# Neighbourhood attention on half key blocks, with the query blocks in the order 1, 2, 0, 3

## The chip, the core and the metric

The kernel runs on one core of a Trainium2 chip. The metric is the device time of one execution in microseconds; the kernel before takes 1600.47 us (median of three runs, 1600.18 to 1600.92).

## What is computed

The reference is an encoder of two layers on 512 tokens of width 1024. In each layer a normed input goes through one combined projection and from there into four branches: a convolution branch, neighbourhood attention (NA), dilated attention and windowed attention; the branches are gated, summed, projected and added back, and a feed-forward part with a small convolution follows. The change touches the second branch. Cut to what matters of it:

```python
def _neighbourhood_attn(q, k, v, rpb):      # grid of 8 rows x 64 columns, 4 heads of 64
    ...
    col_start = np.clip(col - kc // 2, 0, GRID_W - kc)      # kc = 16
    col_idx = col_start[:, None] + np.arange(kc)[None, :]
    ...
        s = jnp.einsum('bwhd,brwkhd->bhwrk', q_r, k_r).astype(jnp.float32) * scale
        s = s + bias[None]
        p = jax.nn.softmax(s.reshape(bsz, heads, GRID_W, kr * kc), axis=-1)
        ...
        return jnp.einsum('bhwrk,brwkhd->bwhd', p, v_r)
```

A query sees the 16 nearest grid columns (clamped at the edges) with all 8 rows of each. The bias depends on the difference of rows and columns and on the head.

## The kernel before

The weights are streamed from memory once, in units of 128 x 1024. Each unit is loaded on the SP queue (`w_raw`, L201), split by ScalarE into a high part (`w_hi`, L204) and by VectorE into a low part (`w_lo`, L206), and multiplied in three products (L225 to L227, or L407 to L409 for projections with tokens on the partitions). There are two buffers for the raw unit and three for each part.

All attention work is put into this stream. The method `tick` is called at fixed places between products, and each call takes one step of the generators that wait in `side`. So TensorE's order is written out by the program: a stretch of weight products, one attention step, the next stretch.

For NA the tokens are kept column by column of the grid, 8 tokens to a column, so a block of 128 queries covers 16 grid columns and its keys lie in the neighbouring columns. `qk_norm` (L460) transposes Q and K and splits K into `KH` and `KL`. `project_v` (L543) evaluates V for two branches; NA's V is written to the DRAM buffer `turn` row by row (L552) and read back in grid order as one tile `Vn` of 1024 KB (L556), called V in the rows.

`attention` (L570) serves three branches. It has 16 items, one for each of 4 heads and 4 query blocks. At step t it does three things:

- `values` (L637), in every second step: for a pair of blocks (`hf`, blocks 0 and 1 or 2 and 3) it multiplies V with the transposed probabilities, a high product (L651) and a low one (L652) for each key block, into one PSUM tile; ScalarE copies the lower half out (L657) and VectorE adds the halves (L658, tile `yf`).
- `transposes` (L619) of item t-3: a transpose for each key block (L628), a copy into `pth` by ScalarE (L634) and the low part `ptl` by VectorE (L635).
- `scores` of item t (L581): two products, Q with `KH` (L591) and with `KL` (L592); VectorE adds the bias and takes the maximum (L605), ScalarE makes the exponential (L609) and the scaled copy (L616).

Score, transpose and value results share four PSUM buffers (`aux`, L219), which are taken in turn. So a score product may have to wait for the reader of a result that was made four buffers earlier.

Key ranges are whole blocks of 128: block i sees the blocks i-1 to i+1, so the inner blocks 1 and 2 have 384 keys and the outer ones 256. In `values` a pair reads three key blocks, the first two by 256 query columns or, for the third, the one block of 128 that sees it. The bias table of a head has 896 columns (L152): 384 that both inner blocks use, and 256 for each outer block. It is loaded into a single buffer `tab` of 448 KB at the head's first score step (L583 to L586):

```python
            if kind == 'na' and i == 0:
                tab = self.ap.tile([P, 896], F32, name="tab", tag="tab", bufs=1)
                nc.sync.dma_start(tab, self.TB[l, h])
                tabs[h] = tab
```

The order of instructions on each engine and queue is fixed when the program is built, and instructions of one engine run in that order.

Of the kernel before, what the change touches and what calls it, by code (L numbers as in the profile page):

```python
# [22 lines left out]
P = 128  # L23
L = 2
D = 1024
S = 512
KT = D // P
NB = S // P
# [117 lines left out]
def na_tables(rpb):  # L146

    c_of = np.arange(S) // 8
    r_of = np.arange(S) % 8
    parts = []  # L150
    pad = np.concatenate([rpb.reshape(L, 4, -1), np.full((L, 4, 1), -BIG, np.float32)], -1)
    for blk, k0, k1 in ((1, 0, 384), (0, 0, 256), (3, 256, 512)):  # L152
        q = blk * P + np.arange(P)
        k = np.arange(k0, k1)
        cq, rq, ck, rk = c_of[q][:, None], r_of[q][:, None], c_of[k][None], r_of[k][None]
        cs = np.clip(cq - 8, 0, 48)
        ok = (ck >= cs) & (ck < cs + 16)
# [23 lines left out]
class Trunk:  # L181
# [361 lines left out]
    def project_v(self, Vn, Vd):  # L543

        vn = [self.ap.tile([P, 2, 4, P], F32R, name=n, tag=n, bufs=2) for n in ("pth", "ptl")]
        turn = self.dram.tile([S // 8, 8, 4 * P], F32, name="turn", tag="turn", bufs=1)

        def evac(b, ps):
            t = vn[b // 2][:, b % 2]
            self.evac_v(t, b, ps[:, :256], 4)  # L550
            for e in range(2):
                self.nc.sync.dma_start(turn[:, 2 * b + e],  # L552
                                       t[64 * e:64 * e + 64].bitcast(F32).rearrange("p h x -> p (h x)"))
            self.evac_v(Vd[:, b], b, ps[:, 256:], 4)
        self.token_major(evac)
        self.nc.sync.dma_start(Vn.bitcast(F32).rearrange("p b h x -> p b (h x)"),  # L556
                               turn.rearrange("(b c) r x -> (c r) b x", b=NB))

    def project_swa(self, V):
        Q = self.new_Q()  # L560
# [9 lines left out]
    def attention(self, l, kind, V, yi):  # L570


        nc = self.nc
        v = nc.vector
        QS, KH, KL = self.qk
        yh, yl = self.y_tiles()
        half = lambda e: slice(64 * e, 64 * e + 64)
        blocks = lambda i: (0, 4) if kind == 'dil' else (max(0, i - 1), min(4, i + 2))
        tabs, yfs, pts = {}, {}, {}

        def scores(h, i):  # L581
            hk = h // 2 if kind == 'swa' else h
            if kind == 'na' and i == 0:  # L583
                tab = self.ap.tile([P, 896], F32, name="tab", tag="tab", bufs=1)
                nc.sync.dma_start(tab, self.TB[l, h])
                tabs[h] = tab  # L586
            k0, k1 = blocks(i)
            n = (k1 - k0) * P
            ps = self.aux()
            q = QS[:, h, i * P:(i + 1) * P]  # L590
            nc.tensor.matmul(ps[:, :n], lhsT=q, rhs=KH[:, hk, k0 * P:k1 * P], start=True, stop=False)  # L591
            nc.tensor.matmul(ps[:, :n], lhsT=q, rhs=KL[:, hk, k0 * P:k1 * P], start=False, stop=True)  # L592
            if kind == 'na':
                o = {0: 384, 3: 640}.get(i, 0)
                bias = tabs[h][:, o:o + n]
# [21 lines left out]
            return e  # L617

        def transposes(h, i, e):  # L619
            hf, u = i // 2, i % 2  # L620
# [3 lines left out]
            k0, k1 = blocks(i)  # L624
            n = (k1 - k0) * P
            ps = self.aux()
            for kb in range(k1 - k0):
# [3 lines left out]
            K0 = 0 if kind == 'dil' else hf  # L631
            ks = slice(k0 - K0, k1 - K0)
            qs = slice(u * P, (u + 1) * P)
            nc.scalar.activation(pth[:, ks, qs], src, AF.Copy)  # L634
            v.tensor_tensor(ptl[:, ks, qs], src, pth[:, ks, qs].bitcast(F32), ALU.subtract)  # L635

        def values(h, hf):  # L637
            hk = h // 2 if kind == 'swa' else h
            pth, ptl = pts.pop((h, hf))
            full = slice(0, 256)  # L640
            if kind == 'dil':
                K0, kbs = 0, [(kb, full) for kb in range(4)]
            else:

                K0, kbs = hf, [(0, full), (1, full), (2, slice(P, 256))]
                if hf == 1:
                    kbs = [(1, full), (2, full), (0, slice(0, P))]
            po = self.aux()
            for n, (kb, qs) in enumerate(kbs):
                vs = V[:, K0 + kb, hk, :]  # L650
                nc.tensor.matmul(po[:, qs], lhsT=vs, rhs=pth[:, kb, qs], start=n == 0, stop=False)  # L651
                nc.tensor.matmul(po[:, qs], lhsT=vs, rhs=ptl[:, kb, qs], start=False, stop=n == len(kbs) - 1)  # L652
            if h % 2 == 0 and hf == 0:
# [4 lines left out]
            v.tensor_tensor(yf[half(h % 2), hf * 256:(hf + 1) * 256], po[0:64, :256], tmp, ALU.add)  # L658
            if h % 2 == 1 and hf == 1:
                j = h // 2  # L660
                s_, oh, ol = yf, yh[:, j, :], yl[:, j, :]
# [3 lines left out]
                nc.scalar.activation(oh, s_, AF.Copy)  # L665
                v.tensor_tensor(ol, s_, oh.bitcast(F32), ALU.subtract)

        items = [(h, i) for h in range(4) for i in range(NB)]
        es, n = {}, len(items)
        for t in range(n + LAG + 2):  # L670
            if t >= LAG + 3 and (t - LAG) % 2 == 1:
                h, i = items[t - LAG - 3]
                values(h, i // 2)
# [198 lines left out]
    def layer(self, l):  # L872
# [3 lines left out]
        with tc.tile_pool(name="gate", bufs=1, reuse_waits="tile") as self.gp:  # L876
            with tc.tile_pool(name="attn", bufs=1, reuse_waits="tile") as self.ap:
                self.scratch = lambda: self.gp.tile([P, S], F32, name="raw", tag="t1", bufs=2)
                late = lambda n: iter([None] * n)
# [100 lines left out]
```

## Time and profile before

| What | Value |
|---|---|
| median of three runs | 1600.47 us (1600.18 to 1600.92) |
| profiled execution, its own time | 1601.61 us |
| its span, first to last instruction | 1599.8 us |
| TensorE busy | 1590.4 us (99%) |
| VectorE busy | 1104.4 us (69%) |
| ScalarE busy | 779.8 us (49%) |
| GpSimd busy | 104.0 us (6%) |
| moved by DMA | 176.01 MB, 110 GB/s on average |

The span is part of the execution's own time. In the rows PE is TensorE's product, PEld its weight load, DVE VectorE, ACT ScalarE, SPq the DMA queue of SyncE. NA lies in two stretches, from about 60 to 130 us in layer 0 and from about 846 to 918 us in layer 1. Records of single products overlap, so a product's price is read from the distance between the starts of neighbours, not from its duration.

### The profile page before, as it was taken

The page shows a single profiled execution, that of the slowest core. Times are in us where ns is not written, and L with a number is a line of the kernel's source. Part 1 is how long each engine was busy: PE and PEld are TensorE (multiplying, and loading weights), DVE is VectorE, ACT ScalarE, POOL GpSimd, SP SyncE. Part 2 cuts the span into 40 slices and gives each one's busy share as a digit, 9 for nine tenths or more (in the row PEclk, how much of TensorE's full clock was granted, in tenths as well). Part 3 has the DMA queues.
Part 4 walks back from the last instruction along what each step waited for, and adds up shares of the span by engine and source line. Part 5 has one row for each costly group of instructions (what it writes and reads, how often), then busy time and mean ns, then how long its engine had stood idle before and what let it go on. Part 6 is the DMA issues. An engine that isn't in the chain of part 4 may idle for free.

```text
span 1599.8 us, 19877 instructions
## 1 busy us (share of the span) xinstructions
PE 1590.4 (99%) x7394; PEld 1323.7 (83%) x7394; DVE 1104.4 (69%) x1845; ACT 779.8 (49%) x1303; POOL 104.0 (6%) x176
## 2 busy tenths in 40 slices
PE   9999999999999999999999999999999999999999
PEld 7888888888888888888888888888888888888887
DVE  6689888765668877843356889887556687777221
ACT  5677766433444444432247777662434444444211
POOL 0012001222000000000000110012210000000000
PEclk9999999999999999999999999999999999999999
DMA  6532222233533333234335322223336332323342
GB/s 217 179 96 87 74 85 80 92 101 96 179 119 105 93 98 100 89 128 130 125 122 184 106 66 85 80 66 106 105 93 188 108 106 93 105 93 91 123 135 73
DMA packets 57489, 176.01 MB, mean 110 GB/s; under 512 B 6960, under 2 KB 7216, under 8 KB 57392
## 3 DMA queue, kind: packets, MB, share of 16 engines
q1 hardware_dynamic: 56512, 173.15, 34.4%
q0 software_dynamic: 448, 1.06, 0.3%
q8 instruction: 58, 0.95, 0.2%
q10 hardware_dynamic: 432, 0.53, 0.1%
q14 instruction: 39, 0.32, 0.1%
HBM read 158.98 MB, written 10.49 MB: 106 GB/s over the span
## 4 chain that ended last, share of the span: by engine, by line
PE 91%; DVE 4%; ACT 3%; DMA 1%; issue 1%; ACTq 0%; DVEq 0%
PE mm L227 25%; PE mm L225 25%; PE mm L226 25%; PE mm L407 2%; PE mm L409 2%; PE mm L408 2%; PE aux L628 1%; DVE w_lo L206 1%; PE aux L652 1%; PE aux L408 1%; PE aux L409 1%; PE aux L591 1%; PE aux L407 1%; PE aux L651 1%; PE aux L592 1%
## 5 line engine op out<-in xcount | busy, mean ns | idle before, releaser
L225 PE MATMUL mm<-xh,w_hi 128*128 128x512 f32 x1280 | 499.9, 391 | 0.0
L227 PE MATMUL mm<-xh,w_lo 128*128 128x512 f32 x1280 | 498.9, 390 | 0.0
L226 PE MATMUL mm<-xl,w_hi 128*128 128x512 f32 x1280 | 498.6, 390 | 0.0
L204 ACT ACTIVATE w_hi<-w_raw 128x1024 fp32r<-128x1024 f32 (+2 forms) x273 | 284.3, 1042 | 406.1 <-PE mm L226 332.0
L206 DVE TENSOR_TENSOR w_lo<-w_raw,w_hi 128x1024 fp32r<-128x1024 f32 (+2 forms) x273 | 329.9, 1209 | 159.1 <-ACT w_hi L204 155.5
L227 PEld LDWEIGHTS mm<-xh,w_lo 128*128 128x128 f32 x1280 | 240.3, 188 | 50.9
L226 PEld LDWEIGHTS mm<-xl,w_hi 128*128 128x128 f32 x1280 | 240.3, 188 | 48.9
L225 PEld LDWEIGHTS mm<-xh,w_hi 128*128 128x128 f32 x1280 | 240.3, 188 | 48.8 <-ACT V L529 0.3
L225 PE MATMUL mm<-fh,w_hi 128*128 128x512 f32 x352 | 136.9, 389 | 0.0
L226 PE MATMUL mm<-fl,w_hi 128*128 128x512 f32 x352 | 136.9, 389 | 0.0
L227 PE MATMUL mm<-fh,w_lo 128*128 128x512 f32 x352 | 136.9, 389 | 0.0
L345 DVE SCALAR_TENSOR_TENSOR cv<-cv,prm 128x512 f32<-128x512 f32 x120 | 94.5, 788 | 0.6
L722 POOL TENSOR_TENSOR mx<-mx,t 128x512 f32<-128x512 f32 x44 | 67.0, 1529 | 422.6 <-DVE t L721 413.7
L810 ACT ACTIVATE fh<-cy 128x512 fp32r<-128x512 f32 x44 | 27.8, 632 | 112.3 <-DVE cy L807 112.3
L764 DVE TENSOR_TENSOR xn<-mm,xr 128x512 f32<-128x512 f32 x32 | 22.1, 691 | 84.3 <-PE mm L227 78.3
L226 PEld LDWEIGHTS mm<-fl,w_hi 128*128 128x128 f32 x352 | 66.1, 188 | 13.8
L225 PEld LDWEIGHTS mm<-fh,w_hi 128*128 128x128 f32 x352 | 66.1, 188 | 13.8
L798 ACT ACTIVATE cy<-U,prm 128x512 f32<-128x512 f32 x88 | 71.1, 810 | 12.8 <-DVE U L795 11.8
L227 PEld LDWEIGHTS mm<-fh,w_lo 128*128 128x128 f32 x352 | 66.1, 188 | 13.6
L407 PE MATMUL mm<-w_hi,xh 128*128 128x512 f32 x192 | 76.3, 397 | 0.2
L795 DVE TENSOR_TENSOR U<-mm,RB 128x512 f32<-128x512 f32 x88 | 60.4, 689 | 22.9 <-PE mm L227 15.5
L692 DVE TENSOR_TENSOR t<-mm,RB 128x512 f32<-128x512 f32 x64 | 44.0, 687 | 46.2 <-PE mm L227 45.8
(144 smaller groups left out, 2306.3 us busy)
## 6 DMA issues: line engine op xcount, KB each, us to landing
w_raw<-W SPq DMA_DIRECT2D x239, 512.0 KB, 3.6
w_raw<-W SPq DMA_DIRECT2D x32, 448.0 KB, 3.3
res<-xn SPq DMA_DIRECT2D x24, 256.0 KB, 2.0
xr<-res SPq DMA_DIRECT2D x24, 256.0 KB, 2.9
tab<-TB SPq DMA_DIRECT2D x8, 448.0 KB, 3.8
KH<-KH SPq DMA_DIRECT2D x20, 128.0 KB, 3.4
KL<-KL SPq DMA_DIRECT2D x20, 128.0 KB, 3.8
xn<-xT SPq DMA_DIRECT2D x8, 256.0 KB, 6.2
```

Of the source, the lines that this page charges most:

```text
L204: w = nc.scalar.activation(hi[:, s], raw[:, s], AF.Copy)
L206: nc.vector.tensor_tensor(lo[:, s], raw[:, s], hi[:, s].bitcast(F32), ALU.subtract)
L225: mm(ps, lhsT=wh, rhs=xh, start=start, stop=False)
L226: mm(ps, lhsT=wh, rhs=xl, start=False, stop=False)
L227: self.last_mm = mm(ps, lhsT=wl, rhs=xh, start=False, stop=stop)
L345: self.after_mm(v.scalar_tensor_tensor(acc, u[:, t:t + S], w(t), acc, ALU.mult, ALU.add))
L407: mm(pss[b], lhsT=self.Xh[k][:, t], rhs=hi[:, s], start=k == 0, stop=False)
L408: mm(pss[b], lhsT=self.Xh[k][:, t], rhs=lo[:, s], start=False, stop=False)
L409: self.last_mm = mm(pss[b], lhsT=self.Xl[k][:, t], rhs=hi[:, s], start=False, stop=k == KT - 1)
L722: (v if n == ORDER[3] and d >= 6 else nc.gpsimd).tensor_tensor(m, m, t, ALU.add)
L795: v.tensor_tensor(u[:, 1:513], ps, self.RB, ALU.mult)
L798: nc.scalar.activation(y, u[:, 1:513], AF.Identity, scale=w(1), bias=self.par('ffn_conv_b', c))
```

## The change

The key range of an inner block shrinks from 384 to the 256 keys that its queries can reach, 64 to 320 for block 1 and 192 to 448 for block 2. These begin in the middle of a key block, so V is also loaded from `turn` in three tiles `Vs` of 128 keys each, shifted by 64, into buffers of the tag `mx` that the gated sum uses later. The blocks are taken in the order 1, 2, 0, 3, and the pairs of `values` are (1, 2) and (0, 3). The bias table is split: 256 columns for the inner blocks (128 KB), 512 for the outer ones (256 KB), each with one buffer, loaded two steps before the first use (for the first head before `qk_norm`). Key ranges are now counted in half blocks of 64 for all three branches; those of the dilated and the windowed branch stay what they were.

```diff
-    for blk, k0, k1 in ((1, 0, 384), (0, 0, 256), (3, 256, 512)):
+    for blk, k0, k1 in ((1, 64, 320), (0, 0, 256), (3, 256, 512)):
...
         self.token_major(evac)
+
+        self.Vs = [self.gp.tile([P, S], F32, name="mx", tag="mx", bufs=8).bitcast(F32R) for _ in range(3)]
+        for b in range(3):
+            self.nc.sync.dma_start(self.Vs[b].bitcast(F32),
+                                   turn[16 * b + 8:16 * b + 24].rearrange("c r x -> (c r) x"))
         self.nc.sync.dma_start(Vn.bitcast(F32).rearrange("p b h x -> p b (h x)"),
                                turn.rearrange("(b c) r x -> (c r) b x", b=NB))
+
+    def na_bias(self, l, h, pair):
+
+        c0, c1 = ((0, 256), (256, 768))[pair]
+        t = self.ap.tile([P, c1 - c0], F32, name=f"tab{pair}", tag=f"tab{pair}", bufs=1)
+        self.nc.sync.dma_start(t, self.TB[l, h][:, c0:c1])
+        self.tabs[h, pair] = t
+
+    def na_first(self, l, wait):
+
+        for _ in range(wait):
+            yield
+        self.tabs = {}
+        self.na_bias(l, 0, 0)
+        self.na_bias(l, 0, 1)
...
-        blocks = lambda i: (0, 4) if kind == 'dil' else (max(0, i - 1), min(4, i + 2))
+        keys = {'na': ((0, 4), (1, 5), (3, 7), (4, 8)), 'dil': ((0, 8),) * 4,
+                'swa': ((0, 4), (0, 6), (2, 8), (4, 8))}[kind]
+
+        pairs = ((1, 2), (0, 3)) if kind == 'na' else ((0, 1), (2, 3))
+
+        place = {'na': ((1, 3, 5), (0, 2, 4, 6)), 'dil': ((0, 2, 4, 6),) * 2, 'swa': ((0, 2, 4), (2, 4, 6))}[kind]
...
-            if kind == 'na' and i == 0:
-                tab = self.ap.tile([P, 896], F32, name="tab", tag="tab", bufs=1)
-                nc.sync.dma_start(tab, self.TB[l, h])
-                tabs[h] = tab
+            if kind == 'na' and h:
+
+                if i == 0 and h < 3:
+                    self.na_bias(l, h + 1, 0)
+                if i == 1:
+                    self.na_bias(l, h, 1)
+            elif kind == 'na' and i == 0:
+                self.na_bias(l, 1, 0)
+            ks = slice(keys[i][0] * 64, keys[i][1] * 64)
+            n = ks.stop - ks.start
...
-            if kind == 'dil':
-                K0, kbs = 0, [(kb, full) for kb in range(4)]
-            else:
-
-                K0, kbs = hf, [(0, full), (1, full), (2, slice(P, 256))]
-                if hf == 1:
-                    kbs = [(1, full), (2, full), (0, slice(0, P))]
+
+            ends = [[keys[i][0] <= k < keys[i][1] for i in pairs[hf]] for k in place[hf]]
+            kbs = sorted(((kb, slice(P * (not e[0]), P * (1 + e[1]))) for kb, e in enumerate(ends)),
+                         key=lambda x: x[1].start - x[1].stop)
             po = self.aux()
             for n, (kb, qs) in enumerate(kbs):
-                vs = V[:, K0 + kb, hk, :]
+                k = place[hf][kb]
+                vs = (V[k // 2] if k % 2 == 0 else self.Vs[k // 2])[:, hk * P:(hk + 1) * P]
...
-        items = [(h, i) for h in range(4) for i in range(NB)]
+        items = [(h, i) for h in range(4) for i in pairs[0] + pairs[1]]
...
-                self.queue(chain(late(3 if l else 5), self.qk_norm(*Q, 4, 4, 0), self.attention(l, 'na', V, 1)))
+                self.queue(chain(self.na_first(l, 3 if l else 5), self.qk_norm(*Q, 4, 4, 0),
+                                 self.attention(l, 'na', V, 1)))
```

## Rows read from the trace of the kernel before

**Rows 1.** The page, busy time of each engine, share of the span and instructions.

```profile
PE 1590.4 (99%) x7394; PEld 1323.7 (83%) x7394; DVE 1104.4 (69%) x1845; ACT 779.8 (49%) x1303; POOL 104.0 (6%) x176
```

**Rows 2.** Timeline of PE around a value step: start us, us, engine, line, operation.

```profile
298.64 0.28 PE L652 MATMUL aux<-ptl,V 128*128 128x256 f32 x1
298.76 0.22 PE L651 MATMUL aux<-pth,V 128*128 128x128 f32 x1
298.82 0.28 PE L652 MATMUL aux<-ptl,V 128*128 128x128 f32 x1
298.94 0.44 PE L225 MATMUL mm<-xh,w_hi 128*128 128x512 f32 x1
299.22 0.40 PE L226 MATMUL mm<-xl,w_hi 128*128 128x512 f32 x1
299.46 0.39 PE L227 MATMUL mm<-xh,w_lo 128*128 128x512 f32 x1
```

**Rows 3.** Timeline of PE, layer 1, a step of three transposes and 384-wide scores.

```profile
879.13 0.49 PE L628 MATMUL aux<-cst,e 128*128 128x128 f32 x3
...
879.81 0.39 PE L225 MATMUL mm<-xh,w_hi 128*128 128x512 f32 x1
```

**Rows 4.** Timeline of PE, layer 1, a step of two transposes and 256-wide scores.

```profile
886.56 0.38 PE L628 MATMUL aux<-cst,e 128*128 128x128 f32 x2
886.69 0.36 PE L591 MATMUL aux<-KH,QS 128*128 128x256 f32 x1
...
887.01 0.40 PE L225 MATMUL mm<-xh,w_hi 128*128 128x512 f32 x1
```

**Rows 5.** Timeline of the weight loads that belong to rows 2.

```profile
298.77 0.19 PEld L652 LDWEIGHTS aux<-ptl,V 128*128 128x128 f32 x1
298.88 0.19 PEld L225 LDWEIGHTS mm<-xh,w_hi 128*128 128x128 f32 x1
298.99 0.19 PEld L226 LDWEIGHTS mm<-xl,w_hi 128*128 128x128 f32 x1
```

**Rows 6.** Chain of waits, eight products of one column: start us, us, what.

```profile
28.78 0.79 PE mm L295 x8
```

**Rows 7.** Chain of waits, the longest piece between 60 and 104 us.

```profile
69.71 6.54 DMA tab<-TB
```

**Rows 8.** Timeline of DVE, a head's first bias-add; in brackets the idle time before it.

```profile
76.41 0.42 DVE L605 CUSTOM_DVE_ANT_0 e<-aux,tab 128x256 f32<-128x256 f32 x1 [1.63 <-DMA tab<-TB]
```

**Rows 9.** Timeline of PE, steps of NA that stop before their score product.

```profile
82.54 0.38 PE L628 MATMUL aux<-cst,e 128*128 128x128 f32 x2
83.51 0.39 PE L591 MATMUL aux<-KH,QS 128*128 128x256 f32 x1 [0.60 <-DVE yf L658]
...
88.49 0.39 PE L591 MATMUL aux<-KH,QS 128*128 128x256 f32 x1 [0.72 <-DVE ptl L635]
...
99.83 0.39 PE L591 MATMUL aux<-KH,QS 128*128 128x256 f32 x1 [0.41 <-DVE yf L658]
...
902.29 0.38 PE L591 MATMUL aux<-KH,QS 128*128 128x256 f32 x1 [0.49 <-DVE mx L605]
```

**Rows 10.** Lines by form, NA's bias-adds: busy us, mean ns | idle before, releaser.

```profile
L605 DVE CUSTOM_DVE_ANT_0 e<-aux,tab 128x384 f32<-128x384 f32 x16 | 8.8, 547 | 1.5 <-PE aux L592 1.5
...
L605 DVE CUSTOM_DVE_ANT_0 e<-aux,tab 128x256 f32<-128x256 f32 x16 | 6.7, 418 | 6.0 <-PE aux L592 4.1 <-DMA tab<-TB 1.9
```

**Rows 11.** Timelines of SP and ACT: a weight load's issue, and the copy that reads it.

```profile
68.43 0.34 SPq L201 DMA_DIRECT2D w_raw<-W  x1
...
80.82 1.05 ACT L204 ACTIVATE w_hi<-w_raw 128x1024 fp32r<-128x1024 f32 x1
```

**Rows 12.** All instructions on the tile w_raw, its loads' time to landing.

```profile
DMA to landing us min/median/max: 3.1/3.5/6.7
```

**Rows 13.** All instructions on the tile V, the loads' time to landing.

```profile
DMA to landing us min/median/max: 5.6/7.1/8.6
```

**Rows 14.** Waits on SP, 55 to 130 us: who waited for whom, us, times, longest.

```profile
SPq L585 <- DVE mx L605: 10.6, 3, 5.3
```

More of the change, by code (lines that the diff above doesn't have):

```diff
@@ L575, in attention @@
         QS, KH, KL = self.qk
+        V = [V[:, b].rearrange("p h x -> p (h x)") for b in range(NB)]
         yh, yl = self.y_tiles()
         half = lambda e: slice(64 * e, 64 * e + 64)
-        blocks = lambda i: (0, 4) if kind == 'dil' else (max(0, i - 1), min(4, i + 2))
-        tabs, yfs, pts = {}, {}, {}
+        keys = {'na': ((0, 4), (1, 5), (3, 7), (4, 8)), 'dil': ((0, 8),) * 4,
+                'swa': ((0, 4), (0, 6), (2, 8), (4, 8))}[kind]
+        pairs = ((1, 2), (0, 3)) if kind == 'na' else ((0, 1), (2, 3))
+        place = {'na': ((1, 3, 5), (0, 2, 4, 6)), 'dil': ((0, 2, 4, 6),) * 2, 'swa': ((0, 2, 4), (2, 4, 6))}[kind]
+        yfs, pts = {}, {}
         def scores(h, i):
             hk = h // 2 if kind == 'swa' else h
-            if kind == 'na' and i == 0:
-                tab = self.ap.tile([P, 896], F32, name="tab", tag="tab", bufs=1)
-                nc.sync.dma_start(tab, self.TB[l, h])
-                tabs[h] = tab
-            k0, k1 = blocks(i)
-            n = (k1 - k0) * P
+            if kind == 'na' and h:
[7 more added lines that the diff above has]
+            n = ks.stop - ks.start
             ps = self.aux()
             q = QS[:, h, i * P:(i + 1) * P]
-            nc.tensor.matmul(ps[:, :n], lhsT=q, rhs=KH[:, hk, k0 * P:k1 * P], start=True, stop=False)
-            nc.tensor.matmul(ps[:, :n], lhsT=q, rhs=KL[:, hk, k0 * P:k1 * P], start=False, stop=True)
+            nc.tensor.matmul(ps[:, :n], lhsT=q, rhs=KH[:, hk, ks], start=True, stop=False)
+            nc.tensor.matmul(ps[:, :n], lhsT=q, rhs=KL[:, hk, ks], start=False, stop=True)
             if kind == 'na':
-                o = {0: 384, 3: 640}.get(i, 0)
-                bias = tabs[h][:, o:o + n]
+                bias = self.tabs[h, 0] if i in (1, 2) else self.tabs[h, 1][:, i // 3 * n:(i // 3 + 1) * n]
             elif kind == 'dil':
@@ L619, in transposes @@
         def transposes(h, i, e):
-            hf, u = i // 2, i % 2
+            hf = i not in pairs[0]
+            u = pairs[hf].index(i)
             if u == 0:
@@ L623, in transposes @@
             pth, ptl = pts[h, hf]
-            k0, k1 = blocks(i)
-            n = (k1 - k0) * P
+            nk = (keys[i][1] - keys[i][0]) // 2
+            n = nk * P
             ps = self.aux()
-            for kb in range(k1 - k0):
+            for kb in range(nk):
                 nc.tensor.transpose(out=ps[:, kb * P:(kb + 1) * P], in_=e[:, kb * P:(kb + 1) * P],
@@ L630, in transposes @@
             src = ps[:, :n].rearrange("p (k q) -> p k q", q=P)
-            K0 = 0 if kind == 'dil' else hf
-            ks = slice(k0 - K0, k1 - K0)
+            k0 = place[hf].index(keys[i][0])
+            ks = slice(k0, k0 + nk)
             qs = slice(u * P, (u + 1) * P)
@@ L639, in values @@
             pth, ptl = pts.pop((h, hf))
-            full = slice(0, 256)
-            if kind == 'dil':
-                K0, kbs = 0, [(kb, full) for kb in range(4)]
-            else:
-                K0, kbs = hf, [(0, full), (1, full), (2, slice(P, 256))]
-                if hf == 1:
-                    kbs = [(1, full), (2, full), (0, slice(0, P))]
+            ends = [[keys[i][0] <= k < keys[i][1] for i in pairs[hf]] for k in place[hf]]
+            kbs = sorted(((kb, slice(P * (not e[0]), P * (1 + e[1]))) for kb, e in enumerate(ends)),
+                         key=lambda x: x[1].start - x[1].stop)
             po = self.aux()
             for n, (kb, qs) in enumerate(kbs):
-                vs = V[:, K0 + kb, hk, :]
+                k = place[hf][kb]
+                vs = (V[k // 2] if k % 2 == 0 else self.Vs[k // 2])[:, hk * P:(hk + 1) * P]
                 nc.tensor.matmul(po[:, qs], lhsT=vs, rhs=pth[:, kb, qs], start=n == 0, stop=False)
@@ L657, in values @@
             nc.scalar.activation(tmp, po[64:128, :256], AF.Copy)
-            v.tensor_tensor(yf[half(h % 2), hf * 256:(hf + 1) * 256], po[0:64, :256], tmp, ALU.add)
+            a, b = pairs[hf]
+            rows = yf[half(h % 2)].rearrange("p (b q) -> p b q", q=P)[:, a:b + 1:b - a]
+            two = lambda t: t.rearrange("p (b q) -> p b q", q=P)
+            v.tensor_tensor(rows, two(po[0:64, :256]), two(tmp), ALU.add)
             if h % 2 == 1 and hf == 1:
@@ L672, in attention @@
                 h, i = items[t - LAG - 3]
-                values(h, i // 2)
+                values(h, i not in pairs[0])
             if LAG <= t < n + LAG:
@@ L878, in layer @@
                 self.scratch = lambda: self.gp.tile([P, S], F32, name="raw", tag="t1", bufs=2)
-                late = lambda n: iter([None] * n)
                 Q = self.project_qk(None, self.aux)
```

## The prediction

> **What bounds the kernel now.** I read the page first, for the engine that fills the span, then the timeline of TensorE and of its weight loads inside the neighbourhood attention (NA), then the chain of waits of the same stretch, and last the SP queue. In the page the reader is to see one thing: TensorE is busy for 1590.4 of 1599.8 us [rows 1]. Every microsecond that leaves TensorE's queue is worth a microsecond, and what VectorE and ScalarE save is worth something only where TensorE waits for them. The durations of single matmuls are no prices, since they overlap: a 512-column product is recorded with about 0.39 us, but the next one starts 0.24 us later [rows 2]. So I price by distances between starts.
>
> The NA runs as steps, one per pair of head and query block, put into the stream of weight products. A step on TensorE is: the two score products of item t, the transposes of item t-3, and in every second step the value products of a pair of blocks. Where nothing waits, steps of one composition repeat within a few ns, 16 items in each of the two layers.
>
> **Part 1, inner blocks on 256 keys instead of 384: fewer transposes and narrower scores.** Compare two undisturbed steps of layer 1. One with three transposes and 384-wide scores takes from 879.13 to 879.81, 0.68 us until the stream goes on; one with two transposes and 256-wide scores takes from 886.56 to 887.01, 0.45 us [rows 3, 4]. The difference, 0.22 us, is exactly what an inner block loses: one transpose and 128 columns in each of two score products. (A step carries the scores of one item and the transposes of another, but over a head the count is the same.) Two inner blocks x 4 heads x 2 layers = 16 items x 0.22 = **-3.5 us**, all on the engine that sets the end.
>
> **Part 2, the value products.** Before, a pair of blocks has three key blocks: two over 256 query columns, one over 128, each as a high and a low product: 4 of 256 and 2 of 128, for both pairs. After, the inner pair (1, 2) has key ranges that meet in one of three places: 2 products of 256 and 4 of 128. The outer pair (0, 3) shares no key at all: 8 products of 128 and none of 256. The columns fall by a fifth, from 2560 to 2048 per head, but the number of products rises from 12 to 14 (the two come from the two transposes saved, so TensorE's instruction count should stay at 7394 [rows 1]). What does a 128-wide product cost? A 256-wide one costs 0.12 us from start to start [rows 2]. The first 128-wide one seems to cost 0.06, the second 0.12, and the stream's next product is then followed after 0.28 instead of 0.24 [rows 2]. The weight loads beside them explain it: they go off 0.11 apart [rows 5], and the next product cannot run before its weights are there. Each product here has its own weight load, and eight products of one single column, each with a load, take 0.79 us, 0.10 each [rows 6]. So a narrow product costs a weight load, 0.11 us, and halving 256 columns saves 0.01, not 0.06. I take 0.113, since rows 2 and 5 are of this very operation. Per head: inner pair 2 x 0.12 + 4 x 0.113 = 0.69 us against 4 x 0.12 + 2 x 0.113 = 0.71; outer pair 8 x 0.113 = 0.90 against 0.71. That is +0.18 per head, **+1.5 us** over eight head passes. The other bound is 0.06 for each narrow product [rows 2]: 0.24 + 12 x 0.06 = 0.96 against 4 x 0.12 x 2 + 4 x 0.06 = 1.20 per head by the same price, -0.24 per head, -1.9 us.
>
> The Trainium skill, "TensorE: Matmul & The Clock Gate", section "LDWEIGHTS (loading the stationary operand)", puts a load at its columns over 1.2 per ns, 107 ns for 128, whatever the product's width; the 0.11 of the weight loads agrees. The same page, section "Back-to-back issue gap", gives about 81 ns for a sustained 128-wide product; that would make this part an estimated -0.6 us (1.21 us against 1.28 per head) instead of +1.5, and the sum about 2 us lower.
>
> **Part 3, the bias tables.** Now a head's table of 448 KB lies in one buffer, so its load starts only when the last block of the head before has read it, in the same step in which the next head needs it. In the chain the load of head 1 stands with 6.54 us, the longest piece of the stretch [rows 7], and VectorE sits idle for 1.63 us of it [rows 8]; behind it ScalarE's exponentials come late, PSUM buffers stay taken, and at 82.54 TensorE's step stops before its score product until 83.51 [rows 9]. An undisturbed step takes 0.13 between these two starts [rows 4], so the stall costs 0.84 us, 0.24 more than the 0.60 listed as idle. Four such stops stand in NA, with 0.60, 0.72, 0.41 and 0.49 us of idle time [rows 9]; with 0.24 each that is about 3.2 us. After the change the loads are 128 and 256 KB, two steps ahead. Two steps take from 879.13 to 886.56, 7.4 us [rows 3, 4], so a load has that against the 6.54 of the slow one. The first stop has the table as its direct cause; the second and third follow within 17 us, while VectorE and ScalarE catch up and also serve the norms of the next Q and K; the last is in layer 1, where a score's bias-add comes late. The bias-add of an inner block also falls from 547 to 418 ns [rows 10], and the low-part subtraction, the exponential and two copies shrink alike, which helps the catching up. I take **-2.5 us** of the 3.2: all of the first and most of the others. Bounds: 0 (the norms alone cause them) and -3.2; above nothing by about 1.5, if the new order puts a burst of two or three steps into the same places.
>
> **Part 4, the half-block copies of V.** Three loads of 256 KB go into the SP queue ahead of the 1024 KB one of V. The inner pair reads only the new copies, the outer pair only V, and the inner pair comes first, so V has two more steps. The weight load behind them is issued at 68.43 and its bytes are first read at 80.82 [rows 11]; weight loads land within at most 6.7 us [rows 12], which leaves 5.7 us. The new loads add three quarters of V's bytes; V takes at most 8.6 us [rows 13], so they delay by at most 6.5 us. I cost them at nothing. If the cover failed, the weight would be late by 0.8 us. The buffers of the copies are those in which the gated sum is kept later, which starts only when NA's output is complete. The strided write of the outer pair's outputs and the changed order of blocks move no work. Dilated and windowed attention get the same key ranges as before, written in half blocks.
>
> **Sum.** -3.5 + 1.5 - 2.5 = -4.5 us. The profiled execution took 1601.61 us (its span 1599.8 and 1.8 around it), 1.1 above the median of the three runs, so it would go to 1597.1; taken from the median 1600.47 the forecast is **1596.0 us**.
>
> **Rivals.** (a) *The stalls stay or move.* The Q and K norms of the dilated branch fall into these very steps, and VectorE's order is fixed beforehand. For it: two of the four stops wait for a sum behind such a burst, not for a table. Against: the first has the table alone. Then the time is 1600.47 - 2.0 = 1598.4, to 1600 if the new order adds a stop of 1.5. Chance 0.27. This is also the case in which the two steps of lead don't do what they say. (b) *Narrow products cost their columns.* For it: the 0.06 after the first one. Against: the weight loads' 0.11 and the one-column products' 0.10. Then part 2 gives -1.9 and the time is 1600.47 - 3.5 - 1.9 - 2.5 = 1592.6. Chance 0.07. (c) *Slower: the SP queue holds a weight load back.* SP works in order, and a table load waits there for the bias-add that frees its buffer, 10.6 us over three loads, 5.3 the longest [rows 14]. There will be about twice as many such loads, each with a weight load behind it. If the longest wait falls on the stretch in which the copies of V already use up the cover, 5.3 + 6.5 - 5.7 = 6.1 us of weights are missing, and with the stalls kept the time is 1600.47 - 2.0 + 6.1 = 1604.6. It decides from a wait plus delay of 5.7 us on. Against: the loads that wait now hide entirely. Chance 0.05.
>
> **How the numbers follow.** My forecast has 0.61, the rivals 0.27, 0.07 and 0.05. A measurement of this kernel can tell about 0.2%, 3.2 us, from no change: up to 1597.3 counts as faster. The forecast lies 1.3 us below that, and a little of it reaches over; with (b) faster has 0.64. Same takes (a) and that edge, 0.31; slower is (c), 0.05. The range takes the stalls from fully gone with a little more (-3.2, and part of the way to (b)) to the upper end of (a): 1593.0 to 1600.2.
>
> **What would show it.** Right: TensorE's count is still 7394; the first narrow product after the last 256-wide one follows as now, but in a run of eight they start 0.11 apart; two-transpose, 256-wide steps of 0.45 us everywhere in NA; no table load in the chain, no idle VectorE behind one; no stop at the steps named. Wrong: narrow products 0.06 apart; stops of the same size in NA or new ones later in the layer; a weight product that waits for its split weights between 65 and 130 us or in layer 1 behind V. A time above 1598 would say that part 3 failed, one below 1593 that part 2's price is too high.

## The result, and the profile after

The changed kernel takes 1602.48 us (median of 22 runs, 1600.72 to 1603.55); the kernel before, timed beside it, 1599.62 us (22 runs, 1599.12 to 1600.92). The ratio is 1.0017 with a 95% interval of 1.001 to 1.0024: slower by 2.9 us, within the 0.2% named above, but clear of its interval and on the other side of the forecast of 1596.0. The profiled execution after took 1603.16 us.

The page after: the span, and busy time of each engine, as in [rows 1].

```profile
span 1601.4 us, 19902 instructions
...
PE 1588.9 (99%) x7394; PEld 1321.3 (83%) x7394; DVE 1100.1 (69%) x1845; ACT 775.4 (48%) x1303; POOL 104.2 (7%) x176
...
PE 87%; DVE 6%; ACT 4%; issue 1%; DMA 1%; ACTq 0%; SPq 0%; DVEq 0%
```

TensorE's instruction count stayed at 7394 and its busy time fell, yet the span grew. The third line is the chain of waits by engine: 13 of 100 parts of it lie outside TensorE, 9 before. So there is less work and more stopping. The steps of the attention show both.

Timeline of PE after, layer 1: first an undisturbed step without values (the one of [rows 4]), then the value products of an outer pair.

```profile
862.35 0.38 PE L659 MATMUL aux<-cst,e 128*128 128x128 f32 x2
862.48 0.36 PE L622 MATMUL aux<-KH,QS 128*128 128x256 f32 x1
...
862.80 0.40 PE L407 MATMUL mm<-w_hi,xh 128*128 128x512 f32 x1
...
875.86 0.23 PE L679 MATMUL aux<-pth,V 128*128 128x128 f32 x1
875.92 0.27 PE L680 MATMUL aux<-ptl,V 128*128 128x128 f32 x1
876.03 0.27 PE L679 MATMUL aux<-pth,V 128*128 128x128 f32 x1
876.14 0.28 PE L680 MATMUL aux<-ptl,V 128*128 128x128 f32 x1
...
876.48 0.27 PE L679 MATMUL aux<-pth,V 128*128 128x128 f32 x1
876.59 0.27 PE L680 MATMUL aux<-ptl,V 128*128 128x128 f32 x1
876.70 0.41 PE L659 MATMUL aux<-cst,e 128*128 128x128 f32 x2
```

The plain step takes 0.45 us, and in the run of eight narrow products the starts lie 0.11 apart after the first 0.06: a half-width product costs its weight load. Parts 1 and 2 came out as worked.

Timeline of PE after, the largest new or longer stops; they answer to [rows 9]. The last is in the dilated attention.

```profile
82.05 0.38 PE L659 MATMUL aux<-cst,e 128*128 128x128 f32 x2
83.59 0.39 PE L622 MATMUL aux<-KH,QS 128*128 128x256 f32 x1 [1.16 <-DVE mx L635]
...
95.21 0.41 PE L659 MATMUL aux<-cst,e 128*128 128x128 f32 x2
96.60 0.39 PE L622 MATMUL aux<-KH,QS 128*128 128x256 f32 x1 [0.98 <-DVE ptl L666]
...
151.96 0.60 PE L659 MATMUL aux<-cst,e 128*128 128x128 f32 x4
154.05 0.50 PE L622 MATMUL aux<-KH,QS 128*128 128x512 f32 x1 [1.49 <-DVE ptl L666]
```

The first stop grew from 0.84 to 1.41 us (1.54 between the two starts, less the 0.13 of a free step).

To add all stops up I took, for each composition of attention steps, the shortest time that any of the kernels needs for it. That is the step's work; what a step takes beyond it is stop. All columns but the first are us of one profiled execution each, the median is that of the timed runs; the second row is the kernel before in another execution (told below).

| Kernel | median | work | stops NA, layer 0 | dilated, 0 | NA, 1 | dilated, 1 | windowed | all stops |
|---|---|---|---|---|---|---|---|---|
| before, as in the rows above | 1599.62 | 109.3 | 2.70 | 0.31 | 1.15 | 1.63 | 1.19 | 6.98 |
| before, profiled again | | 109.3 | 1.02 | 0.29 | 1.11 | 1.62 | 1.17 | 5.22 |
| after | 1602.48 | 107.1 | 3.57 | 1.80 | 1.71 | 2.25 | 1.22 | 10.55 |
| after, V on POOL | 1599.74 | 107.1 | 0.78 | 1.86 | 1.69 | 2.22 | 1.18 | 7.73 |
| before, copies of V on SP | 1602.54 | 109.2 | 2.67 | 0.23 | 1.38 | 1.89 | 1.20 | 7.36 |
| after, V on POOL, wide last pair | 1596.48 | 106.2 | 0.80 | 0.54 | 1.80 | 0.98 | 1.17 | 5.28 |
| after, wide values | 1594.56 | 102.1 | 2.80 | 0.51 | 1.29 | 0.06 | 1.21 | 5.87 |
| after, wide values, V on POOL | 1592.49 | 102.1 | 0.40 | 0.30 | 1.33 | 0.07 | 1.17 | 3.27 |

The work fell by 2.2 us. The stops rose by 5.3 against the second row: 2.6 in NA of layer 0, 1.5 in the dilated attention of layer 0, and 0.6 in each of the two in layer 1. -2.2 + 5.3 = 3.1 us, beside 3.4 between these two spans and 2.9 between the medians. What remains is to find what each stop comes from.

### The profile page after: what moved, and what is told of

The parts are those of the page before. It is cut to its first block, busy times and chain, and to the rows that moved or that the text cites. A ratio compares the mean times of both kernels' runs of the same rounds, so it can differ in the third digit from the quotient of the medians.

```text
span 1601.4 us, 19902 instructions
## 1 busy us (share of the span) xinstructions
PE 1588.9 (99%) x7394; PEld 1321.3 (83%) x7394; DVE 1100.1 (69%) x1845; ACT 775.4 (48%) x1303; POOL 104.2 (7%) x176
## 4 chain that ended last, share of the span: by engine, by line
PE 87%; DVE 6%; ACT 4%; issue 1%; DMA 1%; ACTq 0%; SPq 0%; DVEq 0%
PE mm L225 25%; PE mm L227 25%; PE mm L226 25%; PE mm L407 2%; PE mm L409 2%; PE mm L408 2%; DVE w_lo L206 2%; PE aux L659 1%; ACT w_hi L204 1%; ACT e L639 1%; PE aux L408 1%; PE aux L409 1%; PE aux L407 1%; ACT e L646 1%; DVE cv L345 1%
```

## The experiments

**The kernel before, profiled once more.** The profiled execution of before took 1601.61 us, more than any of its timed runs in this study, so another was taken, with no edit.

> The kernel before, unchanged, profiled once more. The profiled execution on which the prediction rests took 1601.61 us, 2 us more than the median of 22 runs. Theory E: its extra 2 us are stops in NA of layer 0 behind head 1's table, which landed at 76.25; in another execution the table lands before 75, the stop at 82 us is absent and the stops of layer 0's NA come to 0.5 to 1.2 us instead of 2.7, the span to about 1598. Rival: the stops are as long here, the 2 us lie elsewhere.

It took 1599.77 us with a span of 1598.0. Timelines of DVE and PE of this execution, the places of [rows 8] and [rows 9].

```profile
74.10 0.55 DVE L635 TENSOR_TENSOR ptl<-aux,pth 128x384 fp32r<-128x384 f32 x1
74.56 0.41 DVE L605 CUSTOM_DVE_ANT_0 e<-aux,tab 128x256 f32<-128x256 f32 x1
...
82.41 0.38 PE L628 MATMUL aux<-cst,e 128*128 128x128 f32 x2
82.54 0.36 PE L591 MATMUL aux<-KH,QS 128*128 128x256 f32 x1
```

The bias-add of head 1 runs at 74.56 with no idle time before it, instead of 76.41 behind 1.63, and the stop at 82 us does not exist. Theory E holds: layer 0's NA stops for 1.02 us, not 2.70. The 1.7 us between them are most of what that first execution took longer (1601.61 against 1599.77).

**The changed kernel with V's loads on another queue.**

```diff
-            self.nc.sync.dma_start(self.Vs[b].bitcast(F32),
+            self.nc.gpsimd.dma_start(self.Vs[b].bitcast(F32),
...
-        self.nc.sync.dma_start(Vn.bitcast(F32).rearrange("p b h x -> p b (h x)"),
+        self.nc.gpsimd.dma_start(Vn.bitcast(F32).rearrange("p b h x -> p b (h x)"),
```

> The changed kernel with the four loads of V (three shifted copies and V itself) issued on the POOL queue instead of SP's. Theory A: the table of head 1 is late because it stands behind 1.75 MB of V in SP's queue (issued at 69.24, landed at 77.82, VectorE idle for 3.42 us). Then it lands 2 to 4 us earlier, VectorE's idle time behind it falls under 1.5 us, the stop of 1.40 us at 82 us shrinks by at least 0.5 us, and the time falls by 0.5 to 2 us against the changed kernel. Rival B: the stops come from the bursts of the next projection's norms, and the table only stands in front of them: the idle time falls, but the sum of the stops in NA and after it stays within 0.5 us, and so does the time.

1599.74 us, ratio to before 1.0001 (0.9992 to 1.001): 2.7 us less than the changed kernel, a little over theory A's 2. First the timeline of SP in the kernel before, V alone.

```profile
65.28 0.39 SPq L556 DMA_DIRECT2D V<-turn  x1
```

The changed kernel's timeline of SP, and of DVE at the bias-add that waits.

```profile
65.80 0.90 SPq L559 DMA_DIRECT2D mx<-turn  x2
68.38 0.33 SPq L201 DMA_DIRECT2D w_raw<-W  x1
68.76 0.43 SPq L561 DMA_DIRECT2D V<-turn  x1
69.24 1.02 SPq L568 DMA_DIRECT2D tab<-TB  x2
...
77.98 0.43 DVE L635 CUSTOM_DVE_ANT_0 e<-aux,tab 128x256 f32<-128x256 f32 x1 [3.42 <-DMA tab<-TB]
```

Its chain of waits, the longest piece of that stretch, as in [rows 7].

```profile
69.24 8.59 DMA tab<-TB
```

Then the timelines of SP, DVE and PE with V on POOL: the same load, bias-add and step.

```profile
64.89 0.38 SPq L568 DMA_DIRECT2D tab<-TB  x1
...
71.96 0.42 DVE L635 CUSTOM_DVE_ANT_0 e<-aux,tab 128x256 f32<-128x256 f32 x1 [1.70 <-PE aux L623]
...
81.58 0.38 PE L659 MATMUL aux<-cst,e 128*128 128x128 f32 x2
81.72 0.36 PE L622 MATMUL aux<-KH,QS 128*128 128x256 f32 x1
```

In the changed kernel SP issues the copies (the first line has the last two), a weight load that had to wait, V, and only then head 1's table, which lands after 8.59 us although it is no more than 128 KB. In the kernel before, V was issued at 65.28, ahead of that weight load and 4.4 us before head 1's table (69.71 in [rows 7]); here it is issued half a microsecond before it. With V elsewhere the table goes off at 64.89, VectorE waits only for its score product, and the step does not stop; NA's stops in layer 0 fall from 3.57 to 0.78 us. The stops of the dilated attention did not move: theory B keeps those.

**The copies alone, in the kernel before.**

```diff
+        for b in range(3):
+            t = self.gp.tile([P, S], F32, name="mx", tag="mx", bufs=8)
+            self.nc.sync.dma_start(t, turn[16 * b + 8:16 * b + 24].rearrange("c r x -> (c r) x"))
         self.nc.sync.dma_start(Vn.bitcast(F32).rearrange("p b h x -> p b (h x)"),
```

> The kernel before, with the three shifted copies of V loaded ahead of V on SP's queue and not used. Theory A (the queue): V lands later and head 1's table behind it, so VectorE's idle time before that head's first bias-add rises from 1.63 to over 2.5 us and the stop of 0.84 us at 82 us to over 1.2; the time rises by 0.4 to 2 us. Rival: the copies share idle bandwidth and the table lands as before, the time stays within 0.4 us.

1602.54 us, ratio 1.0018 (1.0009 to 1.0027): three loads that nobody reads cost as much as the whole change. The sizes in layer 0 were expected too large against the first profile: head 1's bias-add waits 1.73 us (over 2.5 expected), the stop near 82 us is 0.74 (over 1.2 expected), and NA of layer 0 stops for 2.67 us in all, 1.65 more than in the second profile of before. Layer 1 has its own case. Chain of waits of this kernel in layer 1.

```profile
863.56 0.33 SPq L201
...
863.93 5.07 DMA tab<-TB
```

Here the table stands behind a weight load, which waits for its buffer, and the chain runs through the table's landing into a stopped step.

**A control: V of the kernel before on POOL.**

```diff
-        self.nc.sync.dma_start(Vn.bitcast(F32).rearrange("p b h x -> p b (h x)"),
+        self.nc.gpsimd.dma_start(Vn.bitcast(F32).rearrange("p b h x -> p b (h x)"),
```

> The kernel before with V's load on the POOL queue, a control for the changed kernel with its V loads there, which gained 2.7 us. If the queue hurts only with the copies in it (theory A), this gains little: 0 to 1 us. If V on SP costs the kernel before as much as the changed one, it gains 2 to 3 us.

1600.89 us, ratio 1.0007 (0.9998 to 1.0016): no gain, and by the medians 1.3 us more than the kernel before beside it (1599.55). Its profile has about 1 us more of stops in NA of layer 1, whose cause was not looked for. So the 2.7 us of the changed kernel are not a gain of the POOL queue in itself; the queue hurt because of what the change put into it.

**All tables of the changed kernel loaded early,** into `mx` buffers that lie idle until NA has ended.

```diff
-        self.na_bias(l, 0, 0)
-        self.na_bias(l, 0, 1)
+        mx = lambda: self.gp.tile([P, S], F32, name="mx", tag="mx", bufs=8)
+        for g in range(2):
+            t = mx()
+            for e in range(2):
+                self.nc.sync.dma_start(t[:, 256 * e:256 * e + 256], self.TB[l, 2 * g + e][:, 0:256])
+                self.tabs[2 * g + e, 0] = t[:, 256 * e:256 * e + 256]
...
```

> The changed kernel with the bias tables of all four heads loaded before the NA begins, into buffers that lie idle then; no table load waits for anything and none stands behind V. Theory A (late tables): no idle VectorE in front of a bias-add for a DMA, the NA stops of layer 0 fall from 3.2 us to under 1.2, the time falls by 2 us or more against the changed kernel, to 1600.5 or less beside a kernel before of 1599.6. Rival B (bursts of norms and the fixed order of VectorE and ScalarE): at most the first stop (1.4 us) goes, the stops near 95, 152 and 945 us stay, and the time falls by less than 1.5 us.

NA of layer 0 stops for 0.76 us as theory A wants, and the stops near 152 and 945 us stay as theory B wants (1.76 and 1.29). The median is 1601.26, ratio 1.0009 (1.0 to 1.0017), 1.2 us less than the changed kernel, theory B's side of the bound. The profiled execution was the fastest of its eleven (1599.66); what the others lose is not in a trace.

**The same early tables in the kernel before** (whole blocks, two `mx` tiles per head).

```diff
-                tab = self.ap.tile([P, 896], F32, name="tab", tag="tab", bufs=1)
...
+            for j, (c0, c1) in enumerate(((0, 384), (384, 896))):
+                t = self.gp.tile([P, S], F32, name="mx", tag="mx", bufs=8)
+                self.nc.sync.dma_start(t[:, :c1 - c0], self.TB[l, h][:, c0:c1])
```

> The kernel before (whole blocks, order 0 to 3) with the tables of all four heads loaded before the NA begins. Theory A: the three stops of layer 0 (0.84, 0.97, 0.65 us) follow from the late table of head 1; the first goes and the others shrink, and the time falls by 1 to 2.5 us against the kernel before. Rival B (bursts of norms): the first stop goes at most (0.84 us), the others stay or move, and the time stays within 1 us.

1599.71 us, ratio 1.0002 (0.9993 to 1.001): nothing, and theory A's 1 to 2.5 us were wrong. The second profile of before suggests why: in that execution, which stands near the median, the stop that early tables remove is not there.

**The early loads of the tables undone in the changed kernel:** one table of 384 KB per head, loaded at its first step.

```diff
-                if i == 0 and h < 3:
-                    self.na_bias(l, h + 1, 0)
...
+            if kind == 'na' and i == 1:
+                tab = self.ap.tile([P, 768], F32, name="tab", tag="tab", bufs=1)
+                nc.sync.dma_start(tab, self.TB[l, h])
```

> The changed kernel with the bias tables as before: one table of 384 KB per head in one buffer, loaded at the head's first step. What is left of the change is half blocks and the new order. Theory A: loading two steps ahead gave nothing, since the loads that matter land no earlier: within 1 us of the changed kernel. Rival: the early loads already save something in heads 2 and 3 and in layer 1, and without them the time rises by 1 to 3 us.

1603.75 us, ratio 1.0026 (1.0016 to 1.0035), 1.3 us slower than the changed kernel: the rival's side, though the two intervals touch. In its profile it is NA of layer 1 that stops about 0.7 us longer. So loading ahead is worth about a microsecond, where it isn't undone by the queue.

**Where the dilated attention's stop comes from.** The stop near 152 us is the same 1.75 to 1.80 us in the changed kernel and in its variants with other queues and tables. In the step at 132.7 us the last outer pair of NA and a score of the dilated attention stand together. I lengthened that step in the kernel before.

```diff
+            if kind == 'na' and (h, hf) == (3, 1):
+                kbs = [kbs[0], (2, slice(0, P)), (2, slice(P, 256)), kbs[2]]
```

> The kernel before, with one key block's products of the last NA pair (head 3, blocks 2 and 3) cut into two halves of 128 columns, in both layers: this pair then has 2 products of 256 and 6 of 128 columns, 0.2 us more TensorE time per layer, as much as the outer pair of the changed kernel has there. Theory C: these 0.2 us, in the step that also carries a score of the dilated branch, turn round VectorE's fixed order (split weights ahead of that score's bias-add), and the stop of 1.75 us near 151 us of the changed kernel comes from that. Then the stop near 151 us grows from 0.14 to over 1 us, and the time rises by 1.5 us or more. Rival D: the stop belongs to the half blocks or the order of the blocks: the stop stays under 0.4 us and the time within 0.8 us (0.4 us of it the products).

The stop near 151 us is 0.98 us here (0.10 in the second profile of before), and the median 1601.10, ratio 1.0009 (1.0 to 1.0018), 1.4 us more, 0.4 of it the products. That is theory C's side, just short of its numbers. Timelines of DVE: first the second profile of before, then this kernel. The score's bias-add, ahead of the weights' low part before, now comes behind it.

```profile
133.91 0.68 DVE L605 CUSTOM_DVE_ANT_0 e<-aux,cst 128x512 f32<-128x512 f32 x1
134.52 1.22 DVE L206 TENSOR_TENSOR w_lo<-w_raw,w_hi 128x1024 fp32r<-128x1024 f32 x1
```

```profile
134.68 1.23 DVE L206 TENSOR_TENSOR w_lo<-w_raw,w_hi 128x1024 fp32r<-128x1024 f32 x1 [0.30 <-ACT w_hi L204]
...
136.38 0.69 DVE L605 CUSTOM_DVE_ANT_0 e<-aux,cst 128x512 f32<-128x512 f32 x1
```

The converse: the changed kernel with V on POOL, and only that last pair's products made shorter, by the wide products told of below. With it the high and low parts lie in one tile in every pair, and VectorE has one more addition in that pair.

```diff
+                if kind == 'na' and (h, hf) == (3, 1):
+                    nc.tensor.matmul(po.rearrange("p (s q) -> p s q", s=2)[:, :, qs], lhsT=vs,
+                                     rhs=pt[:, :, kb, qs], start=n == 0, stop=n == len(kbs) - 1)
+                    continue
```

> The changed kernel with V on the POOL queue, and the wide value products in the last outer pair of NA alone (head 3, blocks 0 and 3), in both layers; all other pairs keep the narrow ones. TensorE's work falls by 0.4 us per layer. Theory C (the length of the step that also carries a dilated score turns VectorE's fixed order round): the stop of 1.80 us near 148 us in layer 0 falls under 0.6 us, the time falls by 1.5 to 3 us against 1599.7. Rival D (half blocks and order as a whole): the stop stays over 1.2 us, the time falls by about 0.8 us.

1596.48 us, ratio 0.998 (0.9972 to 0.9989), 3.3 us less than with V on POOL alone, a little over the 1.5 to 3 expected; 0.9 of it is work. Timelines of DVE and PE with V on POOL.

```profile
133.01 1.23 DVE L206 TENSOR_TENSOR w_lo<-w_raw,w_hi 128x1024 fp32r<-128x1024 f32 x1 [0.31 <-ACT w_hi L204]
134.27 0.42 DVE L689 TENSOR_TENSOR yf<-aux,ytmp 64x256 f32<-64x256 f32 x1
134.72 0.69 DVE L635 CUSTOM_DVE_ANT_0 e<-aux,cst 128x512 f32<-128x512 f32 x1
...
148.73 0.60 PE L659 MATMUL aux<-cst,e 128*128 128x128 f32 x4
150.86 0.50 PE L622 MATMUL aux<-KH,QS 128*128 128x512 f32 x1 [1.53 <-DVE ptl L666]
```

The same places with the last pair shortened.

```profile
132.11 0.68 DVE L637 CUSTOM_DVE_ANT_0 e<-aux,cst 128x512 f32<-128x512 f32 x1
...
132.71 1.22 DVE L206 TENSOR_TENSOR w_lo<-w_raw,w_hi 128x1024 fp32r<-128x1024 f32 x1
133.97 0.42 DVE L696 TENSOR_TENSOR yf<-aux,ytmp 64x256 f32<-64x256 f32 x1
...
147.87 0.60 PE L661 MATMUL aux<-cst,e 128*128 128x128 f32 x4
148.61 0.50 PE L624 MATMUL aux<-KH,QS 128*128 128x512 f32 x1
```

With the long pair VectorE's order has the weights' low part and NA's sum ahead of the dilated score's bias-add, which comes 2.6 us later (134.72 against 132.11; the whole stretch is 0.5 later). Some 14 us after, the score product starts 2.13 us after the transposes instead of 0.74. Theory C holds for layer 0: the order was turned round when the kernel was built, and the kernel before has the short order too.

The order is not the whole of it. In the kernels with wide products throughout (below) it is the long one, and the stop is nearly gone. Timelines of PE and DVE of the one with V on SP: the score's second product, the weights' low part, the bias-add.

```profile
130.69 0.39 PE L625 MATMUL aux<-KL,QS 128*128 128x512 f32 x1
...
131.70 1.22 DVE L206 TENSOR_TENSOR w_lo<-w_raw,w_hi 128x1024 fp32r<-128x1024 f32 x1
...
133.40 0.69 DVE L637 CUSTOM_DVE_ANT_0 e<-aux,cst 128x512 f32<-128x512 f32 x1
```

What the stop follows is how late the bias-add starts after that product. Layer 0, us, one profiled execution each:

| Kernel | bias-add and the weights' low part | bias-add after its product | stop near 146 to 151 us |
|---|---|---|---|
| before, profiled again | bias-add first | 1.78 | 0.10 |
| after, V on POOL, wide last pair | bias-add first | 2.39 | 0.41 |
| after, wide values | bias-add last | 2.71 | 0.45 |
| before, longer last pair | bias-add last | 3.65 | 0.98 |
| after | bias-add last | 4.05 | 1.75 |
| after, V on POOL | bias-add last | 4.10 | 1.80 |

In layer 1 the kernel before already has the long order, 4.18 us and a stop of 1.08, and the changed kernel 4.79 and 1.29. So nothing was turned round there, and the shortened pair, with 2.60 and 0.42, gains in layer 1 beyond what the change had cost.

**Wide value products.** The probabilities' high and low part lie side by side in one tile, and one product of twice the width makes both; VectorE adds the halves.

```diff
-                pts[h, hf] = [self.ap.tile([P, 4, 256], F32R, name=n, tag=n, bufs=2) for n in ("pth", "ptl")]
+                pts[h, hf] = self.ap.tile([P, 2, 4, 256], F32R, name="pt", tag="pt", bufs=2)
...
+                if kind == 'na':
+                    nc.tensor.matmul(po.rearrange("p (s q) -> p s q", s=2)[:, :, qs], lhsT=vs,
+                                     rhs=pt[:, :, kb, qs], start=n == 0, stop=n == len(kbs) - 1)
+                    continue
...
+            if kind == 'na':
+                v.tensor_tensor(rows, two(po[0:64, 256:]), rows, ALU.add)
```

The expectation's "Left out: nothing" does not quite hold: the product of V's low part and the probabilities' low part, which the narrow kernels add, is formed here but not added. What adding it would cost was not tried. On the changed kernel, with V on SP as there:

> The changed kernel with the high and low probabilities side by side in one tile, so that a key block's two value products become one of twice the width (256 columns for one query block, 512 for a shared key block): 4 products of 256 for the outer pair, 2 of 256 and one of 512 for the inner one. The two halves are added by one more VectorE addition of 64x256 per pair. Left out: nothing that the high-low scheme keeps. If a narrow product costs a weight load (0.11 us) and a 256-wide one 0.12, TensorE's work in NA falls by 0.65 us per head, 5.2 us in all; the time falls by 3 to 6 us against the changed kernel, less what the longer VectorE work (0.41 us per pair) and a new order of the engines give back. If a narrow product cost its columns (0.06), there would be next to nothing to gain (under 1 us).

1594.56 us, ratio 0.9969 (0.9957 to 0.998), 7.9 us less than the changed kernel: 5.0 of work and 4.7 fewer us of stops in these profiles (1.1 of it is given back outside the attention steps, which was not followed up). That is more than the 3 to 6 expected, since the shorter steps also took away the dilated attention's stops (2.25 to 0.06 in layer 1). With V on POOL as well:

> The kernel of the wide value products with V's loads on the POOL queue. Theory: both gains add, since one is a stop and the other work of TensorE: 2 to 3 us less than with the wide products alone, 1594 to 1597 us beside a kernel before of 1599.7. Rival: VectorE's additional additions bring the stops back, and it stays within 1 us of the kernel before.

1592.49 us, ratio 0.9956 (0.9944 to 0.9969): faster than the kernel before by 7.2 us (1599.66 beside it) and than the changed one by 10.0. The gains add as the theory had it (2.1 us less than with the wide products alone), and the time is 1.5 us below the range expected. Timeline of PE, an outer pair's values and the step after them.

```profile
85.32 0.64 PE L683 MATMUL aux<-pt,V 128*128 128x256 f32 x4
85.80 0.38 PE L661 MATMUL aux<-cst,e 128*128 128x128 f32 x2
```

Four products in 0.48 us do what eight did in 0.84 (875.86 to 876.70 above).

**What half blocks are worth then.** The kernel before with wide values and V on POOL, whole blocks and one table.

> The kernel before (whole blocks, order 0 to 3, one table) with the wide value products and V on the POOL queue. It tells what half blocks and the new order are worth once a narrow value product no longer costs a weight load. TensorE's work: two products of 512 and one of 256 per pair, 0.57 us against 0.71, so 2.2 us less than before; with half blocks it was 7.2 us less (102.1 against 109.3 us of steps). If work decides: 1597 to 1598.5 us, 4 to 6 us more than the half-block kernel with wide products and V on POOL (1592.5). If VectorE's stops decide, the two are within 2 us.

1598.40 us, ratio 0.999 (0.9981 to 0.9999), so 5.9 us more than the half-block kernel with the same two edits. Work decides, as the first reading had it: by the steps in the traces 5.3 us of it is work (5.0 expected). That is what half blocks, the new order and the split tables are worth together once the products are wide. In the change as it was made they saved only 2.2 us of work, and the stops took more than that.

## Why the prediction was wrong

**Parts 1 and 2 were right.** -3.5 + 1.5 = -2.0 us of TensorE's work were forecast, 109.3 to 107.1 measured. The narrow product costs 0.11 us; rival (b) is out. The lower price of about 81 ns, which the Trainium skill, "TensorE: Matmul & The Clock Gate", section "Back-to-back issue gap", gives for a sustained 128-wide product, is not what this stream shows: the starts lie 0.11 apart. They agree with the load time of the same page of the Trainium skill, section "LDWEIGHTS (loading the stationary operand)", which works out to an estimated 107 ns for 128 columns.

**Part 3 failed, first in its base.** "Four such stops ... about 3.2 us" came from one execution that was slower than its median, and I took the sum from the median all the same. In the second profile the stops at 82 and 88 us are absent, NA of layer 0 stops for 1.02 us in all, and the two stops that are left (near 97 and 900 us) come to 1.5 us. So 2.5 us were not there to be had in such an execution; the early tables in the kernel before gained nothing. NA's stops in both layers, 2.13 us there, rose to 5.28 instead of falling. And the two that were left are not the table's: in the changed kernel with V on POOL no bias-add waits for a table, and they stand at 0.62 and 0.81 us beside 0.70 and 0.83 in the kernel before. The gap of profile and median was in the prediction (1.1 us above the three runs), and should have been a warning about the terms that depend on when a load lands.

**Part 4 failed in what stands behind a load.** "I cost them at nothing" looked at the weight load behind V, which indeed was never late by what was feared. But the next head's table stands behind V too. The change puts 768 KB in front of V, and V itself falls behind a weight load that waits for its buffer (68.76 instead of 65.28). So the table that was to come two steps early was issued at 69.24, hardly earlier than before (69.71; with V on POOL 64.89), and landed 8.59 us later. The two parts were costed apart, and the one undid the other. The copies alone in the kernel before cost 2.9 us, and taking V off SP in the changed kernel gave 2.7 back. Rival (c) had the place, SP's order, but the wrong victim, and so a chance of 0.05.

**Rival (a) was the nearest,** with its added stop: 1.5 us in the dilated attention of layer 0, and part of the 0.6 in layer 1. It was forecast for NA. It came behind NA, since two more narrow products in one step turned round VectorE's order of two other things in layer 0.

So the account by the profiles is: work -2.2, the queue +2.6 in NA of layer 0 (2.7 and 2.9 by the medians of its two experiments), the dilated attention's stops +2.1, and 0.6 in NA of layer 1; together 3.1, beside 2.9 between the medians. The 0.6 lies nearly all in a stop near 890 us, which neither V on POOL nor the wide products removed. Timelines of DVE and PE after show what it waits for: a low part that stands behind four products of the next Q's norm.

```profile
888.91 2.50 DVE L457 TENSOR_TENSOR Q<-Q,r_y 128x512 f32<-128x512 f32 x4
891.33 0.41 DVE L666 TENSOR_TENSOR ptl<-aux,pth 128x256 fp32r<-128x256 f32 x1
...
891.80 0.39 PE L622 MATMUL aux<-KH,QS 128*128 128x256 f32 x1 [0.33 <-DVE ptl L666]
```

That is a burst of norms, as rival (a) had it. It is read from the trace alone; no experiment moved it, nor the 0.6 of the dilated attention in layer 1 by itself.

## What to carry to other kernels

Before a stop in a trace is counted as a gain, see that the profiled execution stands at the median, and profile again if it doesn't; here it was a stop behind a landing DMA that differed. When loads are added to a queue, list everything behind them that somebody waits for, also what the same change moves there, and read how busy the DMA engines are in that stretch, not over the whole span. Where products carry their own weights, make them wide enough to cover the weight load, by laying parts that share the weights side by side.

## What was not expected

Three loads of 256 KB that nobody reads cost 2.9 us, although the queue's transfers take only a third of the 16 engines' time over the span. That mean hides the stretch: in the changed kernel the engines are busy for 82, 94 and 87% of the three stretches of 3 us from 69 to 78 us. They are as busy with V on POOL (95 to 99% from 65 to 75 us), but there the table goes ahead of V (64.89 against 65.37) and no bias-add waits for it. So in a stretch as busy as this one it counted which transfer came first.

And 0.2 us more TensorE work in a single step per layer (two more products) cost 1.4 us, while taking 0.4 us per layer out of the same step gave 3.3. Only 0.4 and 0.9 of these are the work itself; the rest comes from a bias-add on another engine, whose order is fixed when the kernel is built and which the edit moves. Why the order came out as it did is not shown by any run.
